# A transformer layer on one core: scans a block later, the second norm in steps, FFN's first blocks by halves

## The chip, the cores and the metric

The kernel runs on one core of one Trainium2 chip. The time is that of one execution on the device in microseconds (us). TensorE (PE) multiplies matrices, VectorE (DVE), ScalarE (ACT) and GpSimd (POOL) work element by element, and SyncE (SP) issues DMA transfers. Each has an in-order queue of its own, and a semaphore makes one wait for another.

## What is computed

One layer for 1024 latent tokens with a context of 256, width 1024, in fp32. The shift, scale and gate vectors come from a matrix `w_ada`.

```python
hc = modulate(rms_norm(ctx, norm1_gain), csh1, csc1)
feats_c, post_c = mixer_inputs(hc, w_in, mlstm_gate_bias, None)
ret_c, ml_c, st_f, st_b = bidirectional_scans(feats_c, log_gamma, zero, zero)
hx = modulate(rms_norm(x, norm1_gain), sh1, sc1)
feats_x, post_x = mixer_inputs(hx, w_in, mlstm_gate_bias, rope)
ret_x, ml_x, _, _ = bidirectional_scans(feats_x, log_gamma, st_f, st_b)
x = x + g1 * mixer_output(ret_x, ml_x, *post_x, w_ret_up, w_ml_up, w_out)
x = x + g2 * swiglu(modulate(rms_norm(x, norm2_gain), sh2, sc2), w_ffn_in, w_ffn_out)
return rms_norm(x, final_gain)
```

`bidirectional_scans` runs four retention heads and four mLSTM heads over chunks of 128 tokens, forwards and backwards. In the mLSTM scan, running sums and maxima of the gates i and log sigmoid(f) give three weights per token. `mixer_output` normalises each head's output, gates it, lifts both branches to the full width, merges them and applies `w_out`.

## The kernel before, in words

**Arithmetic.** Each fp32 operand is split into a high and a low part (ACT cast, L191; DVE subtraction, L192), and a product takes three matmuls. A PSUM bank holds 128x512. TensorE has two banks "ch", two "ts" for large products and four "sc" for small ones. Large products come in blocks of 256 weight columns by 1024 tokens. A Winograd scheme takes seven instead of eight quarter products (`winograd_block`, L276, seven steps); weight factors are made by POOL, DVE and ACT from `raw` tiles loaded by SP.

**Stages.** First the vectors from `w_ada` beside the first norm of the context (`scaled_tile`, L468) and the key and value products of the context (`ctx_tiles`, L442: four pairs of weight tiles, eight steps k each). `modulate_split` (L394) makes each tile of a norm twice: on ACT into the high part (L395), on POOL as the full value `tmp` (L396). DVE subtracts them into the low part (L397). Then 14 head blocks (u = 1 to 7 in two parts, u = 0 is plain) and 8 blocks of the merge gates (`wbg`) run in `run_blocks` (L320), which calls `tick` (L994) after each of a block's seven steps. `tick` moves generators on, registered with `beside(generator, rate)`; the rate is the number of yields a tick. They are `gates` (L691, the weights per token; it starts at u = 1), `scan(u)` (L805, one head; the first at u = 2, the last two in gate blocks 1 and 3), `ada2` (L972) and `load_y_ret` (L1059).

**A scan** is a list of slots. `load` fetches a chunk's keys and values (once per direction, 19 loads of 128 KB a scan), `decay` weights them on POOL (L838), `advance` (L852, L857) adds their product to the state, `stage_a`, `stage_b` and `stage_c` make the outputs of chunk j (L898 to L931) into tiles `o`. The squares of `o` are summed on ACT into a scratch tile `junk` (L933), `norm_y` (L941) normalises, `put_y` (L947) transposes and stores.

**After the scans.** Up products (L111 to L113), then the out product by halves of the tokens, `hf` 0 and 1, each followed by its second norm. Then the FFN: two plain blocks for group 0 (`w0` gate, `w1` up), with `right_factors` (L1161, L1166) on DVE for the Winograd blocks in between, then 20 Winograd blocks and the last product. POOL multiplies up by silu of gate into `hid` (L1158), and SP stores it (L1159) for the last product.

The program is written in this order, and the framework orders each engine's instructions from it.

## Time and profile before

| | |
|---|---|
| median of 3 runs | 1650.39 us (1649.82 to 1653.24) |
| profiled execution | 1655.51 us, span 1653.7 us |
| TensorE busy | 1578.3 us, 95% |
| DVE, ACT, POOL busy | 1003.5, 725.7, 460.2 us |
| mean granted clock of TensorE | 0.984 |

The span runs from the first instruction to the last; the execution's own time is 1.8 us longer. TensorE is busy in nearly all of it; from 740 to 900 us and from 1040 to 1500 us its matmuls follow one another without a gap.

### The profile page before, as it was taken

What the parts mean: (1) busy time and instruction counts of PE and PEld (TensorE: products, weight loads), DVE (VectorE), ACT (ScalarE), POOL (GpSimd) and SP (SyncE); (2) the same over time, 40 slices, a digit from 0 to 9 for tenths busy, and PEclk for the clock granted to TensorE, in tenths of its full rate; (3) what the DMA queues carried; (4) which work ended last, traced back from release to release, by engine and by line L of the source; (5) the groups of instructions that cost most, each with busy time, mean ns of one, the idle gap of its engine ahead of it and who ended that gap; (6) DMA issues with size and microseconds to landing.
All of it is one profiled execution on the core that took longest, in us unless ns stands there. A gap on an engine that the chain in (4) does not pass through costs nothing.

```text
span 1653.7 us, 22635 instructions
## 1 busy us (share of the span) xinstructions
PE 1578.3 (95%) x7478; PEld 1287.9 (78%) x7478; DVE 1003.5 (61%) x1841; ACT 725.7 (44%) x1404; POOL 460.2 (28%) x506
## 2 busy tenths in 40 slices
PE   7999978899999999999999999999999999999997
PEld 2677757787878788778888777888888888888886
DVE  4578786776767767765445677555555555536243
ACT  4655434544545566655223354434443334534230
POOL 0143216455344444410220226222222221001001
PEclk9999978999999999999999999999999999999998
DMA  8753537787767765546456312222232224835531
GB/s 293 255 159 104 167 105 234 252 258 240 248 210 218 228 202 180 187 141 215 154 162 202 122 56 96 81 92 84 85 96 87 77 90 155 271 96 179 171 96 52
DMA packets 188230, 264.55 MB, mean 160 GB/s; under 512 B 19232, under 2 KB 85920, under 8 KB 188112
## 3 DMA queue, kind: packets, MB, share of 16 engines
q1 hardware_dynamic: 186240, 260.99, 49.8%
q10 hardware_dynamic: 1872, 2.10, 0.4%
q8 instruction: 59, 0.97, 0.2%
q14 instruction: 59, 0.48, 0.1%
HBM read 206.64 MB, written 56.38 MB: 159 GB/s over the span
## 4 chain that ended last, share of the span: by engine, by line
PE 51%; POOL 2%; DVE 2%; DMA 1%; ACT 1%; issue 0%; DVEq 0%; SPq 0%; ACTq 0%
PE ch L258 15%; PE ts L258 12%; PE ch L1291 2%; PE ch L1292 2%; PE ch L1290 2%; PE ts L1290 2%; PE ts L1292 2%; PE ts L1291 2%; POOL hid L1158 1%; PE ts L113 1%; PE ch L113 1%; PE ts L112 1%; PE ts L111 1%; PE ch L111 1%; PE ch L112 1%; POOL xf L396 1%
## 5 line engine op out<-in xcount | busy, mean ns | idle before, releaser
L192 DVE TENSOR_TENSOR fw<-raw,fw 128x512 fp32r<-128x512 f32 x305 | 223.1, 737 | 156.6 <-ACT fw L191 156.1
L258 PE MATMUL ts<-A,fw 128*128 128x512 f32 x1200 | 300.7, 398 | 1.8 <-DVE A L397 0.9
L191 ACT CAST fw<-raw 128x512 fp32r<-128x512 f32 x305 | 188.0, 620 | 257.2 <-PE ch L1292 89.0
L258 PE MATMUL ch<-A,fw 128*128 128x512 f32 x1176 | 289.4, 394 | 0.0
L258 PEld LDWEIGHTS ts<-A,fw 128*128 128x128 f32 x1200 | 225.1, 191 | 50.9 <-DVE A L397 3.0
L258 PE MATMUL ch<-t,fw 128*128 128x512 f32 x1008 | 250.4, 396 | 5.5 <-ACT u L293 3.9
L258 PEld LDWEIGHTS ch<-A,fw 128*128 128x128 f32 x1176 | 219.5, 189 | 45.8 <-issue 1.0
L258 PEld LDWEIGHTS ch<-t,fw 128*128 128x128 f32 x1008 | 187.5, 189 | 44.7 <-ACT u L293 5.1
L1158 POOL TENSOR_TENSOR hid<-hid,sg 128x512 f32<-128x512 f32 x44 | 90.2, 2062 | 217.6 <-DVE hid L288 200.9
L258 PE MATMUL ts<-t,fw 128*128 128x512 f32 x504 | 129.6, 404 | 3.2 <-ACT fw L191 1.9
L293 ACT COPY u<-ch 128x512 f32<-128x512 f32 x104 | 60.9, 586 | 134.0 <-PE ch L258 133.7
L258 PEld LDWEIGHTS ts<-t,fw 128*128 128x128 f32 x504 | 95.6, 193 | 23.1 <-ACT fw L191 2.1
L192 DVE TENSOR_TENSOR fw<-stg,fw 128x512 fp32r<-128x512 f32 x126 | 94.5, 750 | 31.3 <-ACT fw L191 31.2
L230 POOL TENSOR_TENSOR stg<-raw,raw 128x512 f32<-128x512 f32 x42 | 63.5, 1513 | 156.2 <-DVE fw L192 100.4
L191 ACT CAST fw<-stg 128x512 fp32r<-128x512 f32 x126 | 78.6, 624 | 59.4 <-DVE stg L230 29.2
L838 POOL TENSOR_SCALAR vs<-kv,dcol 128x128 f32<-128x128 f32 x72 | 63.0, 882 | 63.1 <-DMA kv<-kv_d 33.0
L838 POOL TENSOR_SCALAR vs<-kv,colq 128x129 f32<-128x129 f32 x72 | 54.8, 762 | 78.5 <-PE sc L852 38.0
L1282 POOL TENSOR_SCALAR cp<-cp,cpack 128x256 f32<-128x256 f32 (+1 forms) x6 | 8.2, 1361 | 222.1 <-ACT stg L1336 222.1
L192 DVE TENSOR_TENSOR fw<-s,fw 128x512 fp32r<-128x512 f32 x42 | 33.4, 796 | 48.0 <-ACT fw L191 48.0
L983 DVE SCALAR_TENSOR_TENSOR acc<-stg,silu_c,acc 128x512 f32<-128x512 f32 x56 | 46.8, 836 | 18.2 <-DMA stg<-wada 18.1
L230 DVE TENSOR_TENSOR stg<-raw,raw 128x512 f32<-128x512 f32 x42 | 39.0, 930 | 27.1 <-DMA raw<-wffn 16.8
L396 POOL TENSOR_SCALAR t<-stg,a,sh 128x512 f32<-128x512 f32 (+1 forms) x24 | 27.3, 1144 | 95.8 <-issue 31.5
(362 smaller groups left out, 2973.3 us busy)
## 6 DMA issues: line engine op xcount, KB each, us to landing
raw<-wffn SPq DMA_DIRECT2D x88, 256.0 KB
raw<-wfo SPq DMA_DIRECT2D x88, 256.0 KB
kv<-kv_d SPq DMA_DIRECT2D x152, 128.0 KB
raw<-win SPq DMA_DIRECT2D x64, 256.0 KB
stg<-wada SPq DMA_DIRECT2D x64, 256.0 KB
hid_d<-hid SPq DMA_DIRECT2D x44, 256.0 KB
hraw<-hid_d SPq DMA_DIRECT2D x40, 256.0 KB
araw<-wada SPq DMA_DIRECT2D x32, 256.0 KB
```

What stands on the lines that cost most here:

```text
L191: nc.scalar.copy(hi, x)
L192: nc.vector.tensor_tensor(out=lo, in0=x, in1=hi.bitcast(F32), op=ALU.subtract)
L230: eng.tensor_tensor(out=o, in0=x, in1=y, op=op)
L258: nc.tensor.matmul(ps, lhsT=w[wp_][:, c], rhs=x[xp][k], start=start and k == i == 0, stop=cont or (stop and k == 3 and i == 2), skip_group ...
L293: nc.scalar.copy(o, chain)
L396: nc.gpsimd.tensor_scalar(out=tmp, in0=xn, scalar1=scale, scalar2=shift, op0=ALU.mult, op1=ALU.add)
L838: nc.gpsimd.tensor_scalar(out=vs, in0=kv[d, n][1], scalar1=col, scalar2=None, op0=ALU.mult)
L983: nc.vector.scalar_tensor_tensor(out=acc, in0=raw, scalar=s, in1=acc, op0=ALU.mult, op1=ALU.add)
L1158: nc.gpsimd.tensor_tensor(out=c, in0=c, in1=sgs[f, hf], op=ALU.mult)
L1290: nc.tensor.matmul(ps, lhsT=w[0][:, c], rhs=h[0][:, t], start=kt == 0, stop=False)
L1291: nc.tensor.matmul(ps, lhsT=w[0][:, c], rhs=h[1][:, t], start=False, stop=False)
L1292: nc.tensor.matmul(ps, lhsT=w[1][:, c], rhs=h[0][:, t], start=False, stop=kt == 2 * NG - 1)
```

## The change

The diff, cut to its core (`after` and `at` put a function at the end or the start of a scan's slot):

```diff
-    def modulate_split(xn, hi, lo, scale, shift, tmp):
+    def modulate_split(xn, hi, lo, scale, shift, tmp, beneath=False):
         nc.scalar.activation(hi, xn, AF.Identity, scale=scale, bias=shift)
-        nc.gpsimd.tensor_scalar(out=tmp, in0=xn, scalar1=scale, scalar2=shift, ...)
+        if beneath:
+            nc.scalar.activation(tmp, xn, AF.Identity, scale=scale, bias=shift)
+        else:
+            nc.gpsimd.tensor_scalar(out=tmp, in0=xn, scalar1=scale, scalar2=shift, ...)
...
-    ctx_order = [(p, k) for k in range(KT) for p in range(2)] + [(p, k) for p in (2, 3) for k in range(KT)]
+    ctx_order = ([(p, k) for k in range(6) for p in range(2)] + [(2, 0), (2, 1)] + [(p, k) for k in (6, 7) for p in range(2)]
+                 + [(2, k) for k in range(2, KT)] + [(3, k) for k in range(KT)])
...
-                    ctx_ps[pair, n] = mm_ps()
+                    ctx_ps[pair, n] = sc_ps() if pair == 2 else mm_ps()
...
+    for k_ in (0, 1):
+        ctx_tiles(2, (k_,))
+        ctx_load()
     for k_ in (6, 7):
         for pair in range(2):
             ctx_tiles(pair, (k_,))
...
-        nc.gpsimd.tensor_tensor(out=gi, in0=gi, in1=bb, op=ALU.subtract)
-        nc.gpsimd.tensor_tensor(out=bb, in0=bb, in1=m, op=ALU.subtract)
+        nc.vector.tensor_tensor(out=gi, in0=gi, in1=bb, op=ALU.subtract)
...
+        nc.vector.tensor_tensor(out=bb, in0=bb, in1=m, op=ALU.subtract)
...
+        for i, n in enumerate((0, 1, 9, 8, 7, 6, 5, 4, 3, 2)):
+            after(i // 2 if i < 9 else 6, load, n)
         for i, n in enumerate((1, 0, 9, 8, 7, 6, 5, 4, 3)):
-            after(i // 2, load, 1, n)
-            at(i // 2 + 2, decay, 1, n)
-            at(i // 2 + 3, advance, 1, n)
-        for n in range(NCH):
-            after(5 + n, load, 0, n)
-            if n < 9:
-                at(7 + n, decay, 0, n)
-                at(8 + n, advance, 0, n)
+            at(i // 2 + 3, decay, 1, n)
+            at(i // 2 + 4, advance, 1, n)
+        for n in range(9):
+            at(4 + n if n < 2 else 7 + n, decay, 0, n)
+            at(6 + n if n < 2 else 8 + n, advance, 0, n)
...
-            junk = bt([P, P], "junk", 1)
-            nc.scalar.activation(junk, raw, AF.Square, accum_out=ssq[:, j:j + 1])
+            nc.scalar.activation(po[:, 3 * P:], raw, AF.Square, accum_out=ssq[:, j:j + 1])
...
-            at(9 + j, stage_a, j)
-            at(10 + j, stage_b, j)
-            at(11 + j, stage_c, j)
-        at(20, norm_y)
-        at(23, put_y, 0)
-        at(24, put_y, 4)
+            at(10 + j, stage_a, j)
+            at(11 + j, stage_b, j)
+            at(12 + j, stage_c, j)
+        at(21, norm_y)
+        at(25, put_y, 0)
+        at(26, put_y, 4)
...
+    def norm_steps(hf, acc):
+        nc.vector.tensor_tensor(out=acc[0], in0=acc[0], in1=acc[1], op=ALU.add)
+        dg_ = rms_cols(acc[:1], 512)
+        yield
+        y = rms_bcast(dg_)
+        h2 = (slot_a(), slot_a())
+        hh.append(h2)
+        for kt in range(KT):
+            xr = xf[hf][:, kt, :]
+            nc.vector.tensor_tensor(out=xr, in0=y, in1=xr, op=ALU.mult)
+            modulate_split(xr, h2[0][:, kt, :], h2[1][:, kt, :], a2[:, kt:kt + 1], mod2[:, 8 + kt:9 + kt], xr)
+            if kt % 2:
+                yield
...
+                next(norm, None)
+        norm = norm_steps(hf, acc)
+    for _ in norm:
+        pass
...
+        if gidx == 0:
+            held_back.append((hid_d[f, hf], c))
+        else:
+            nc.sync.dma_start(hid_d[2 * gidx + f, hf], c)
...
+                while part == 1 and held_back:
+                    nc.sync.dma_start(*held_back.pop(0))
...
-    plain_block(w0, b_all, plain_copy("sg", lambda f, hf, c: gate_done(sgs, f, hf, c)))
+    plain_half(w0, b_all, 0, gate_copy)
+    plain_half(w1, b_all, 0, up_copy)
     for k in range(4):
         right_factors(k)
     seven_blocks = list(ffn_blocks())
+    plain_half(w0, b_all, 1, gate_copy)
     seven_blocks[0][0].load()
-    plain_block(w1, b_all, plain_copy("hid", lambda f, hf, c: up_done(0, sgs, f, hf, c)))
+    plain_half(w1, b_all, 1, up_copy)
```

Not in this cut: `gates` loads and biases the forget gates before the input gates and has some 23 yields instead of 18; the rates and starts (gates at u = 1, part 1, rate 1 for 0.85; scans from u = 3, rate 1.5 for 1.45, the last three in gate blocks 0, 2 and 4; `ada2` 0.68 for 0.95; `load_y_ret` at block 7, rate 1.6, for block 6, rate 1); a chunk is loaded once for both directions (10 loads a scan instead of 19) and the mask once in each mLSTM scan; tile "kv" has 9 buffers for 8, "sf" 4 for 3, "acc" 4 for 2; one more tile `wx` for the last weights of `w1`.

Three places show how it moves instructions. VectorE at the gates, before (L724 and L725 are the gates' scans; L582 and L579 belong to the rotation of keys and queries; fw, stg and s are weight parts):

```order
L582 SCALAR_TENSOR_TENSOR kt_1947<-wt_1953,kt_1947 128x512
L192 TENSOR_TENSOR fw_1980<-raw_1796,fw_1980 128x512
L192 TENSOR_TENSOR fw_2134<-raw_1983,fw_2134 128x512
L230 TENSOR_TENSOR stg_2137<-raw_1985,raw_1987 128x512
L230 TENSOR_TENSOR s_2142<-stg_2137,raw_1983 128x512
L192 TENSOR_TENSOR fw_2139<-stg_2137,fw_2139 128x512
L724 SCALAR_TENSOR_TENSOR g_1576<-g_1575,g_1574 4x1280
L725 SCALAR_TENSOR_TENSOR g_1573<-g_1574,g_1572 4x1280
L724 SCALAR_TENSOR_TENSOR g_1576<-g_1575,g_1574 4x256
L725 SCALAR_TENSOR_TENSOR g_1573<-g_1574,g_1572 4x256
L724 SCALAR_TENSOR_TENSOR g_1576<-g_1575,g_1574 4x1024
L725 SCALAR_TENSOR_TENSOR g_1573<-g_1574,g_1573,g_1572 4x1024
```

VectorE after the change at the same place, from the second half of the scans on (L755 and L757 are the scans, L764 and L768 POOL's two subtractions of before, L294, L593 and L594 a rotation):

```order
L597 SCALAR_TENSOR_TENSOR kt_1931<-wt_1937,kt_1931 128x512
L757 SCALAR_TENSOR_TENSOR g_1543<-g_1544,g_1543,g_1542 4x1024
L769 COPY gm_1549<-g_1543 4x9
L770 COPY gm_1549<-g_1543 4x1
L764 TENSOR_TENSOR g_1542<-g_1542,g_1546 36x1280
L771 COPY gm_1549<-g_1543 4x1
L772 COPY gm_1549<-g_1543 4x7
L768 TENSOR_TENSOR g_1546<-g_1546,g_1543 36x1280
L294 TENSOR_TENSOR kt_2027<-ts_2014,u_1916 128x512
L774 TENSOR_TENSOR g_1544<-g_1546,gm_1549 36x1280
L593 TENSOR_TENSOR kt_2027<-kt_2027,rp_2029 128x512
L294 TENSOR_TENSOR kt_2055<-ts_1978,wt_2053 128x512
```

The rotation sum L582 (now L597) and four of the instructions for weights that stood ahead of the first scan have gone behind it; between the scans and the sum kt_2055 stand the wide gate products.

TensorE at the first products of a scan's states, before (L852 the state product, L258 a step of a Winograd block):

```order
L258 MATMUL ch_2155<-t_1401,fw_2152 128x512
L258 MATMUL ch_2155<-t_1400,fw_2152 128x512
L258 MATMUL ch_2155<-t_1431,fw_2152 128x512
L258 MATMUL ch_2155<-t_1432,fw_2152 128x512
L852 MATMUL sc_2304<-vs_2257,kv_2220 128x128
L258 MATMUL ch_2155<-t_1431,fw_2152 128x512
L852 MATMUL sc_2307<-vs_2259,kv_2222 128x128
L564 MATMUL sc_2330<-cpack,kt_2204 128x128 x4
L852 MATMUL sc_2341<-vs_2310,kv_2246 128x128
L258 MATMUL ch_2155<-t_1478,fw_2152 128x512
L852 MATMUL sc_2344<-vs_2312,kv_2248 128x128
L258 MATMUL ch_2155<-t_1479,fw_2152 128x512
```

and after (L882 the state product, L265 the block):

```order
L265 MATMUL ts_2446<-t_1293,fw_2314 128x512
L265 MATMUL ts_2446<-t_1312,fw_2314 128x512
L265 MATMUL ts_2446<-t_1313,fw_2314 128x512
L265 MATMUL ts_2446<-t_1312,fw_2314 128x512
L882 MATMUL sc_2460<-vs_2422,kv_2365 128x128
L882 MATMUL sc_2463<-vs_2424,kv_2363 128x128
L882 MATMUL sc_2474<-vs_2466,kv_2395 128x128
L882 MATMUL sc_2477<-vs_2468,kv_2397 128x128
L265 MATMUL ch_2330<-t_1355,fw_2319 128x512
L265 MATMUL ch_2330<-t_1356,fw_2319 128x512
L265 MATMUL ch_2330<-t_1355,fw_2319 128x512
L265 MATMUL ch_2330<-t_1395,fw_2319 128x512
```

A state product stood by itself between two matmuls of a chain, and now several stand together between two chains.

SyncE's queue at the start of the FFN, before (raw are weight loads, hid_d the stores of hid, cp loads of x):

```order
L211 DMA raw_10352<-wffn 128x512
L1159 DMA hid_d<-hid_10197 128x512
L1325 DMA cp_13478<-x_d 128x512
L1325 DMA cp_13480<-x_d 128x512
L1325 DMA cp_13482<-x_d 128x512
L1325 DMA cp_13484<-x_d 128x512
L1159 DMA hid_d<-hid_10226 128x512
L211 DMA raw_10354<-wffn 128x512
L1159 DMA hid_d<-hid_10255 128x512
L211 DMA raw_10356<-wffn 128x512
```

and after:

```order
L211 DMA raw_10110<-wffn 128x512
L1236 DMA hid_d<-hid_9843 128x512
L1236 DMA hid_d<-hid_9871 128x512
L1378 DMA cp_13240<-x_d 128x512
L1378 DMA cp_13242<-x_d 128x512
L1378 DMA cp_13244<-x_d 128x512
L1378 DMA cp_13246<-x_d 128x512
L211 DMA raw_10112<-wffn 128x512
L1236 DMA hid_d<-hid_10015 128x512
L211 DMA raw_10114<-wffn 128x512
```

Two hid stores stand between the first and the second of these weight loads in both.

## Rows read from the trace of the kernel before

**Rows 1.** Windows: length, busy us (x) of PE, PEld, DVE, ACT, POOL, clock, DMA, GB/s.
```profile
216.00:231.50 15.50, 6.16 (x17) 4.50 (x15) 15.41 (x14) 3.58 (x5) 7.03 (x3) 0.67 0.02 3
238.00:245.00 7.00, 7.00 (x32) 5.72 (x32) 3.23 (x5) 4.15 (x15) 0.00 (x0) 0.51 0.47 128
261.00:266.00 5.00, 4.56 (x16) 3.70 (x17) 1.40 (x3) 0.17 (x1) 1.97 (x3) 0.66 1.05 381
272.00:279.00 7.00, 6.21 (x21) 5.45 (x22) 5.24 (x10) 1.93 (x4) 5.34 (x5) 0.51 0.82 262
```

**Rows 2.** Waits of PE, 40 to 120 us: for whom, us in total, times, longest.
```profile
PE ts L452 <- DVE fw L192: 1.9, 2, 1.2
PE ts L451 <- ACT t L395: 1.1, 1, 1.1
```

**Rows 3.** Groups of ScalarE by form: busy us, mean ns | idle before.
```profile
L395 ACT ACTIVATE A<-stg,sh,a 128x512 fp32r<-128x512 f32 x16 | 12.7, 814 | 7.9 <-DVE stg L473 7.8
```

**Rows 4.** Timeline of PE, 216 to 245 us: start, us, what, [idle before].
```profile
225.29 0.32 PE L768 MATMUL sc<-cpack,g 36*128 36x36 f32 x1 [8.91 <-POOL g L736]
...
236.43 0.89 PE L768 MATMUL sc<-cpack,g 36*128 36x36 f32 x11 [1.36 <-ACT g L751]
```

**Rows 5.** Timeline of VectorE, 200 to 240 us.
```profile
205.78 1.78 DVE L582 SCALAR_TENSOR_TENSOR kt<-wt,kt 128x512 f32<-128x512 f32 x1
...
211.05 2.81 DVE L724 TENSOR_TENSOR_SCAN g<-g,g 4x1280 f32<-4x1280 f32 x1 [0.23 <-DMA g<-ls_d]
...
219.96 2.31 DVE L725 TENSOR_TENSOR_SCAN g<-g,g,g 4x1024 f32<-4x1024 f32 x1
...
231.14 1.48 DVE L741 TENSOR_TENSOR g<-g,gm 36x1280 f32<-36x1280 f32 x1
```

**Rows 6.** Waits of PE, 255 to 320 us.
```profile
PE sc L947 <- DVE o L941: 3.5, 1, 3.5
PE sc L852 <- POOL vs L838: 2.2, 1, 2.2
PE ts L258 <- ACT fw L191: 1.9, 1, 1.9
PE sc L898 <- DMA qk<-qk_d: 1.5, 1, 1.5
```

**Rows 7.** Waits of PE, 320 to 722 us.
```profile
PE sc L947 <- DVE o L941: 5.9, 4, 1.8
PE sc L922 <- DVE sf L857: 4.7, 4, 2.6
PE sc L915 <- DVE sf L857: 3.6, 3, 1.4
```

**Rows 8.** Line 933 on ScalarE, the squares: ns min/median/max, and a releaser.
```profile
L933 ACT ACTIVATE junk<-o x64: 293/311/323, 279.0 to 714.4; 128x128 f32<-128x128 f32 x64
...
  POOL o L931: 17.3, 21
```

**Rows 9.** Line 931 on POOL, the gate product.
```profile
L931 POOL TENSOR_TENSOR o<-o,g x32: 454/460/892, 511.8 to 713.9; 128x128 f32<-128x128 f32 x32
```

**Rows 10.** Waits of PE, 900 to 1040 us.
```profile
PE ch L258 <- ACT u L293: 3.4, 1, 3.4
PE ts L113 <- DVE fw L192: 3.3, 1, 3.3
PE ts L258 <- DVE A L397: 0.9, 3, 0.3
PE ts L258 <- ACT A L395: 0.7, 1, 0.7
```

**Rows 11.** Chain that ended last, 905 to 1030 us: start, length, what.
```profile
992.18 21.54 POOL hid L1158 x3
...
1014.15 5.83 DMA raw<-wffn
```

**Rows 12.** Line 1158 on POOL: ns min/median/max, first and last start.
```profile
L1158 POOL TENSOR_TENSOR hid<-hid,sg x44: 1290/1696/18119, 992.2 to 1397.7; 128x512 f32<-128x512 f32 x44
```

More of the change, by code (lines that the diff above doesn't have):

```diff
@@ L212, in raw_quads, with plain_quads @@
         return r
-    def plain_quads(src):
+    def plain_quads(src, last=None):
         r = raw_quads(src)
-        return {k: parts_of(r[k]) for k in ("a11", "a21", "a12", "a22")}
+        w = {k: parts_of(r[k]) for k in ("a11", "a21", "a12")}
+        if last is None:
+            w["a22"] = parts_of(r["a22"])
+        else:
+            split(*last, r["a22"])
+            w["a22"] = last
+        return w
     class Factors:
@@ L708, in gates @@
         yield
-        log_sigmoid(pg, lso, lsx, [P, 80], "g")
-        nc.sync.dma_start(ls_d[1], lso)
-        for d in range(2):
-            nc.sync.dma_start(gf[32 * d:32 * d + H], rows[1][4 * d:4 * d + H])
+        biased(0, gi, gil)
         m, rm = gil, gfl
@@ L717, in gates @@
         nc.gpsimd.memset(rm[32:36, P - 1::P], 0.0)
+        yield
+        yield
+        yield
+        log_sigmoid(pg, lso, lsx, [P, 80], "g")
+        yield
+        nc.sync.dma_start(ls_d[1], lso)
+        for d in range(2):
+            nc.sync.dma_start(gf[32 * d:32 * d + H], rows[1][4 * d:4 * d + H])
+        yield
+        yield
         yield
@@ L783, in open_scans @@
         t = {}
-        t["mask"] = pb.tile([P, 2, P], F32, name="mask")
-        nc.sync.dma_start(t["mask"], a["mask"])
         t["g128"] = pb.tile([P, 2, H], F32, name="g128")
@@ L1022, in first @@
             def first():
-                if (u, part) == (1, 0):
-                    beside(gates(), 0.85)
-                if part == 0:
+                if part == 1:
                     return
-                if u == 2:
+                if u == 1:
+                    beside(gates())
+                if u == 3:
                     drain()
@@ L1030, in first @@
                     open_scans()
-                    beside(ada2(), 0.95)
-                if u >= 2:
-                    beside(scan(u - 2), 1.45)
+                    beside(ada2(), 0.68)
+                if u >= 3:
+                    beside(scan(u - 3), 1.5)
             return w, first, lambda: winograd_block(w, b_all, t_all, head_done(u, part), head_tile, snap_tile)
@@ L1112, in body @@
     hh = []
+    def norm_steps(hf, acc):
+        nc.vector.tensor_tensor(out=acc[0], in0=acc[0], in1=acc[1], op=ALU.add)
+        dg_ = rms_cols(acc[:1], 512)
+        yield
+        y = rms_bcast(dg_)
[6 more added lines that the diff above has]
+            if kt % 2:
+                yield
+    norm = iter(())
     out_w = ahead([a["wout"][i, kh] for _ in range(2) for i in range(4) for kh in range(2)])
     for hf in range(2):
-        acc = [px0.tile([P, 512], F32, tag="acc", bufs=2, name=nm("acc")) for _ in range(2)]
+        acc = [px0.tile([P, 512], F32, tag="acc", bufs=4, name=nm("acc")) for _ in range(2)]
         for i in range(4):
@@ L1200, in body @@
     w0 = plain_quads(a["wffn"][0, 0])
-    w1 = plain_quads(a["wffn"][0, 1])
+    wx = pe.tile([P, 2, 512], F32R, name="wx")
+    w1 = plain_quads(a["wffn"][0, 1], (wx[:, 0, :], wx[:, 1, :]))
     def plain_copy(tag, done):
```

113 lines of the change are left out of this document (57 added, 56 removed).

## The prediction

> **What bounds the kernel now.** TensorE is the bound, so the time changes only by what it loses to waits and to the lower clock. I read three views in this order. First the windows: they show stretches in which its busy time is short or the granted clock is near 0.5, the lower of the two levels (1.2 of 2.4 GHz), at which the same matmuls take twice as long [rows 1]. Half the time spent at that level is lost; the window at 261 us, for one, loses (1 - 0.66) x 5.0 = 1.7 us, and four more stretches of the same length, 3.4 us, begin at 64, 313, 931 and 1023 us. Then the waits of TensorE, by stage: who is late, how often, how long [rows 2, 4, 6, 7, 10]. Then the other engines' own rows at each place [rows 3, 5, 8, 9, 12] and the chain that ended last [rows 11]. A wait costs its own length plus half of the lower-clock stretch that follows it. Matmul work is the same before and after: no matmul is added or removed.
>
> All sums are made against the profiled execution, 1655.51 us. It stands 5.1 us above the median of the three runs (1650.39 us); a gain in the one is taken as the same gain in the other.
>
> **First norm and context products.** Before, TensorE waits 1.9 + 1.1 us for the first norm's tiles and the casts beside it [rows 2]. Behind the wait of 1.1 us lies the slow stretch at 64 us, 1.7 lost. The four context products (12 matmuls) moved ahead stand exactly behind that 1.1 us wait and cover it: 2.8 us back. Against that, ScalarE now makes the norm's tiles: 16 of 128x512 at 0.81 us [rows 3] (13 us) and 8 of 128x256, shorter than 0.81 each, in one queue with the weight casts for which TensorE already waited. POOL is relieved, but TensorE waited here for none of its products directly. I take 2 us of later casts. Bounds: nothing late (0) and half of the 13 us (6.5). **Net 1 us gained** (-4 to +3).
>
> **Gates.** In the window at 216 us TensorE works 6.2 of 15.5 us: 9.3 us idle, of which 8.9 are the wait for POOL's subtraction L736 [rows 1, 4]. The work after it, 225.3 to 231.2, is at half clock (3.0 us lost), then 1.4 us wait for an exponential of ScalarE [rows 4], then a second slow stretch, 7.0 us at 0.51 (3.4 us lost) [rows 1]. Sum 17.1 us. VectorE made the gates' six scans from 211.05 to 222.27 (219.96 + 2.31), 11.2 us without a gap [rows 5], and POOL's subtraction came after them. The change loads the forget gates first and takes both POOL subtractions to VectorE, where the nearest row with the same shape is 1.48 us [rows 5]. By the order, a rotation sum (L582, 1.78 us [rows 5]) and four instructions for weights (0.7 each, by the gap from it to the first scan) no longer stand ahead of the scans, so these begin 4.6 us earlier, near 206.5, if their loads have landed. But between the scans and the sum kt that the next transposes need, VectorE now has 11.2 + three wide products of 1.5 + four of 0.7 (rotation, kt itself among them) + 0.6 of small copies = 19 us: ready near 225.5, where TensorE arrives near 216.4 (225.29 - 8.91 [rows 4, 5]). So the wait changes its name rather than going: 8 to 9 us and one slow stretch of 3, against 17.1. **5 us gained.** Bounds: scans no earlier (211.05 + 19 = 230: 0 gained) and everything hidden but 3 us (14).
>
> **Onset of the scans.** Between 255 and 320 us the waits sum to 3.5 + 2.2 + 1.9 + 1.5 = 9.1 us [rows 6]; the slow stretches in the window at 261, in that at 272 (half of 6.2 busy us at 0.51) and at 313 lose 1.7 + 3.1 + 1.7 = 6.5 us [rows 1]. In total 15.6. After, scans begin one block later, key/value chunks are loaded once in the first slots, and a decay has three slots from the load instead of two; the small products come in groups of 3 or 4 between whole 12-chains instead of one between two matmuls. DMA has 80 loads of 128 KB instead of 152; their cost beside other work was nothing but the 1.5 us wait for a load [rows 6]. **14 us gained**, leaving 1.6 us. Bounds 8 and 15.6.
>
> **Scans, steady part.** From 320 to 722 us the three largest waits are for normalised outputs (5.9 us) and states (4.7 + 3.6 us), 14.2 together [rows 7]. Output waits had three slots between norm and transposes and get four, and the states have one slot and one buffer more. I count 9 of the 14.2 back. Against it stands the squares' new destination: the last quarter of the accumulator bank in place of a scratch tile. The bank now stays held for the square (0.3 us [rows 8]) and, in the four mLSTM scans, for POOL's gate product before it (0.46 us [rows 9]), for which ScalarE waited 0.8 us on average (17.3 us in 21 [rows 8]): 0.8 to 1.6 us longer for 32 mLSTM chunks, 0.3 us and a copy's wait for 32 retention chunks. Scans have four such banks, so most of it lies beside other products; I take 6 us, a fifth of 32 x 1. **Net 3 us gained.** Bounds +14 (no bank waited for) and -23 (each of 32 chunks waits 1 us, 9 back).
>
> By the Trainium skill (ScalarE: Activation LUTs, section "Step-by-step: what each stage is for"), PSUM is ScalarE's lower-latency destination, useful only if TensorE doesn't need most of PSUM. No row here shows the first half; the kernel gives TensorE two "ch", two "ts" and four "sc" banks, so its caveat speaks against this edit and for the third rival.
>
> **Between scans and second norm.** The retention outputs come back one block later at a higher rate; no wait stood there. **1 us lost** (0 to 3).
>
> **Second norm of half 0.** At 930 us a wait of 3.3 us [rows 10] and a slow stretch of 1.7: 5.0 us. Spread over the other half's eight steps, nothing waits for it until the FFN. The casts and multiplies go beside matmuls that last far longer. **5 us gained** (3 to 5).
>
> **FFN's first blocks by halves.** The second half's norm tiles have the first half's up product as cover, so the waits for A (0.9 + 0.7 us [rows 10]) go. The larger loss is later: POOL's first multiply of hid started at 992 and three of them took 21.5 us on the chain [rows 11], where the median of this line is 1.7 and the longest 18.1 [rows 12]; VectorE ran the right factors without a gap meanwhile. The hid stores stand on SP's queue ahead of a weight load (5.8 us), so TensorE waits 3.4 us [rows 10, 11] and loses 1.7 in the slow stretch behind it. The order of SP after the change still has two hid stores ahead of that load, and VectorE's run is the same, so the stall stays, and I allow 2 to 3 us of added wait because half 1's gate product now follows the norm as well. **Net 1 us lost.** Bounds: -3 and +7 (1.6 + 3.4 + 1.7 gone).
>
> The Trainium skill (SBUF — State Buffer, section "SBUF: two separate sides") says that VectorE with two SBUF inputs and GpSimd exclude each other for a whole instruction. The trace agrees where it shows it, 18.1 against 1.7 us for one instruction [rows 12]. If POOL came in between all the same, hid would be out in time and the 7 us would come.
>
> **Sum.** 1 + 5 + 14 + 3 - 1 + 5 - 1 = 26 us. The profiled execution would be 1655.5 - 26 = 1629.5 us; the median 1650.4 - 26 = **1624.4 us**.
>
> **Rivals.** (1) *The edits pay in full*: gates 14, scans 14, FFN 7, the rest as above: 1 + 14 + 14 + 14 - 1 + 5 + 7 = 54, less what no change can hide (two waits of 2 us and their clock, about 8): 46, or 1604 us. For it: every single wait named is one the change addresses. Against it: VectorE's queue at the gates and SP's order at the FFN. Chance 0.17. (2) *The waits are replaced*: casts late in the first norm (-4), gates 0, onset 8, steady part -8, FFN -3, norm 5, -1: 26 shrinks to about -3, and by parts between -3 and 10, or 1640 to 1653 us. For it: the same engines do the same work with more queued behind ScalarE and VectorE. Against it: the onset's single interleaved products clearly go. Chance 0.15. (3) *The held bank decides*: the squares in PSUM. If a chunk's chain to its square is longer than TensorE takes to come back to that bank, TensorE waits in each of the 32 mLSTM chunks. Without the 6 us counted for it the gain is 32, so 1.0 us each (32 x 1.0) uses it up. At 1.5 us each it is 48, and a slow stretch of 1.7 us after a fifth of them adds 11: 1650.4 - 32 + 59 = 1677 us. For it: the bank is held 0.8 to 1.6 us longer. Against it: four banks rotate. Chance 0.08. (4) *The held-back stores do not do what their name says*: this is in the forecast, since the order still has them ahead of the load; if they were behind it, 8 us more would come (7 in place of -1), or 1616; chance 0.05, within the forecast's 0.60.
>
> **How the numbers follow.** Chance of the forecast 0.60, its own range 1614 to 1636 (gates +-5, onset -5, steady part -6 to +5). The rivals 0.17, 0.15 and 0.08. The range 1600 to 1648 takes in most of the first two rivals and leaves out the third and the ends of these two, about 0.18. 0.2% is 3.3 us, about what a measurement of this kernel can tell from no change: faster by more than that 0.85 (forecast, rival 1 and half of rival 2), within it 0.05, slower 0.10 (rival 3 and the end of rival 2).
>
> **What would show it.** In the profile after: at 255 to 320 us no clock near 0.5 and waits under 3 us in sum (right), or waits for vs and o again (wrong). At the gates a wait of TensorE for kt of VectorE of 5 to 9 us in place of the 8.9 for POOL; if it is for POOL or gone, that step is wrong. In the scans no waits for o; a wait of the small products for the square, at more than 0.3 us a chunk, would be rival 3. At 930 clock 1.0 throughout. At the FFN the POOL multiply of hid again near 18 us and a wait for u of 3 to 6 us. In the first norm, waits for a cast. A time above 1648 would mean that waits have moved rather than gone; below 1600, that VectorE's queue at the gates was no limit.

## The result and the profile after

The changed kernel takes 1640.11 us (median of 4 runs, 1636.75 to 1641.78), the one before 1651.81 us on the same chip (median of 4, 1649.82 to 1653.24). The ratio is 0.9919, 95% interval 0.9903 to 0.9935: faster, by 11.7 us in the medians, where 26 were forecast. The forecast of 1624.4 us was too low by 15.7; the measured time lies in the stated range, 1600 to 1648. The profiled execution has a span of 1638.1 us against 1653.7 before, 15.6 us less. That is 4 us more than the medians give: the profiled execution of before, 1655.51 us, was 3.7 us slower than its median of four. The forecast had taken a gain in the one as the same gain in the other.

The stages of both, as windows (length, busy us (x count) of PE, PEld, DVE, ACT, POOL, clock, DMA share, GB/s). Before:

```profile
200.00:250.00 50.00, 39.31 (x170) 31.27 (x169) 40.91 (x49) 20.17 (x42) 11.88 (x8) 0.83 0.38 120
250.00:340.00 90.00, 79.43 (x412) 66.78 (x411) 63.76 (x122) 40.88 (x91) 52.70 (x54) 0.92 0.75 240
340.00:720.00 380.00, 360.92 (x2006) 306.50 (x2004) 270.93 (x651) 207.18 (x485) 167.50 (x285) 1.00 0.68 212
900.00:940.00 40.00, 36.62 (x155) 29.21 (x155) 28.09 (x52) 16.42 (x26) 9.25 (x8) 0.96 0.33 110
940.00:1060.00 120.00, 114.68 (x492) 91.89 (x491) 80.91 (x128) 51.94 (x88) 44.20 (x20) 0.99 0.28 89
```

After:

```profile
200.00:250.00 50.00, 40.36 (x195) 32.68 (x194) 43.04 (x53) 23.30 (x46) 12.46 (x9) 0.90 0.52 155
250.00:340.00 90.00, 78.50 (x399) 65.01 (x398) 62.09 (x117) 41.49 (x90) 46.25 (x48) 0.96 0.70 216
340.00:720.00 380.00, 367.41 (x2042) 312.03 (x2041) 268.32 (x640) 209.31 (x488) 162.49 (x251) 1.00 0.64 194
900.00:940.00 40.00, 40.00 (x181) 32.85 (x179) 29.04 (x55) 18.17 (x29) 8.58 (x8) 1.00 0.43 132
940.00:1060.00 120.00, 114.32 (x488) 92.81 (x487) 83.01 (x129) 53.65 (x92) 51.20 (x21) 0.97 0.25 77
```

What TensorE loses in a window is its idle time (length less busy) and what the clock takes, (1 - clock) x length; the clock has two digits, so the second is good to some tenths of a microsecond in the short windows and not at all in the one of 380 us, which has no slow stretch to speak of in either.

| us lost | before | after | gained | forecast |
|---|---|---|---|---|
| gates, 200 to 250 | 10.7 + 8.5 | 9.6 + 5.0 | 4.6 | 5 |
| onset, 250 to 340 | 10.6 + 7.2 | 11.5 + 3.6 | 2.7 | 14 |
| scans, 340 to 720 | 19.1 | 12.6 | 6.5 | 3 |
| second norm, 900 to 940 | 3.4 + 1.6 | 0 | 5.0 | 5 |
| FFN's start, 940 to 1060 | 5.3 + 1.2 | 5.7 + 3.6 | -2.8 | -1 |

The forecast's window for the onset ended at 320; it is 340 here, because the scans now begin a block later and what follows their start reaches to 335. In the first 120 us the loss falls by 1 to 2 us (11.8 + 1.2 to 11.5), where 1 was forecast. All terms but one came out within a few us. The onset gave 3 us in place of 14. In a second profile of the changed kernel (the first run below) the onset loses 13.5 us and the scans 15.3, so these two gains are 2.7 to 4.3 and 3.8 to 6.5 us. Where the border lies matters: by the forecast's own windows, 255 to 320 and 320 to 722 us, about 8 us are gained in the first and 1 in the second, because a wait of 4 us at 329 us then counts with the scans. Together it is 8 to 9 us either way, where 17 were forecast.

TensorE's waits after, in three stretches, set beside those of [rows 4], [rows 6] and [rows 7]. Between 200 and 250 us:

```profile
PE ch L265 <- ACT wt L299: 9.6, 1, 9.6
```

Between 250 and 340 us:

```profile
PE sc L882 <- DVE wt L979: 4.1, 1, 4.1
PE sc L946 <- DVE W L930: 2.8, 2, 2.6
PE sc L882 <- POOL vs L868: 2.1, 2, 1.7
PE sc L579 <- DVE kt L294: 1.3, 1, 1.3
```

Between 340 and 720 us:

```profile
PE sc L882 <- DVE sf L887: 3.8, 3, 1.7
PE sc L952 <- DVE W L932: 2.4, 4, 0.7
...
PE sc L944 <- DVE sf L887: 1.1, 1, 1.1
...
PE sc L975 <- DVE o L969: 0.2, 1, 0.2
```

Of the waits of the onset before [rows 6], those for the load of queries, for o and for weight casts have gone. In their place TensorE waits 4.1 us for VectorE's product in a store of outputs (L979) and 2.8 for a weighted product W (L930); the wait for vs is still there, 2.1 us in two where it was 2.2 in one. Along the scans, in the forecast's window, the waits for o have fallen from 5.9 to 0.2 us and those for states from 8.3 to 4.9 (L882 and L944). That is the 9 us for which the extra slot and buffer were counted; no run takes these two away by themselves.

### The profile page after: what moved, and what is told of

Read it like the earlier page. It is cut to its first block, busy times and chain, and to the rows that moved or that the text cites. A ratio compares the mean times of both kernels' runs of the same rounds, so it can differ in the third digit from the quotient of the medians.

```text
span 1638.1 us, 22335 instructions
## 1 busy us (share of the span) xinstructions
PE 1571.9 (96%) x7478; PEld 1282.6 (78%) x7478; DVE 999.9 (61%) x1843; ACT 740.6 (45%) x1430; POOL 427.2 (26%) x444
## 4 chain that ended last, share of the span: by engine, by line
PE 63%; DVE 8%; DMA 6%; issue 4%; ACT 3%; POOL 3%; SPq 0%; DVEq 0%; POOLq 0%; ACTq 0%
PE ch L265 20%; PE ts L265 15%; PE ch L1345 2%; PE ch L1344 2%; PE ch L1343 2%; PE ts L1343 2%; PE ts L1345 2%; PE ts L1344 2%; DMA stg<-wada 2%; PE ch L113 1%; PE ts L113 1%; PE ch L111 1%; PE ts L112 1%; PE ch L112 1%; PE ts L111 1%
## 5 line engine op out<-in xcount | busy, mean ns | idle before, releaser
L192 DVE TENSOR_TENSOR fw<-raw,fw 128x512 fp32r<-128x512 f32 x304 | 225.0, 745 | 145.9 <-ACT fw L191 145.1
L265 PE MATMUL ts<-A,fw 128*128 128x512 f32 x1200 | 295.3, 394 | 0.6 <-DVE kt L294 0.6
L265 PE MATMUL ch<-A,fw 128*128 128x512 f32 x1152 | 282.1, 393 | 9.6 <-ACT wt L299 9.6
L265 PE MATMUL ch<-t,fw 128*128 128x512 f32 x1008 | 254.2, 400 | 7.1 <-ACT u L299 5.5
L265 PEld LDWEIGHTS ts<-A,fw 128*128 128x128 f32 x1200 | 222.4, 188 | 46.4 <-DVE kt L294 1.6
L265 PEld LDWEIGHTS ch<-A,fw 128*128 128x128 f32 x1152 | 214.9, 188 | 55.2 <-ACT wt L299 10.2
L265 PEld LDWEIGHTS ch<-t,fw 128*128 128x128 f32 x1008 | 189.9, 191 | 47.4 <-ACT u L299 6.8
L1201 POOL TENSOR_TENSOR hid<-hid,sg 128x512 f32<-128x512 f32 x44 | 95.5, 2182 | 214.9 <-DVE hid L294 202.4
L299 ACT COPY u<-ch 128x512 f32<-128x512 f32 x104 | 60.8, 585 | 147.9 <-PE ch L265 147.8
L265 PE MATMUL ts<-t,fw 128*128 128x512 f32 x504 | 126.8, 399 | 0.0
L192 DVE TENSOR_TENSOR fw<-stg,fw 128x512 fp32r<-128x512 f32 x126 | 95.2, 755 | 40.2 <-ACT fw L191 39.9
L265 PEld LDWEIGHTS ts<-t,fw 128*128 128x128 f32 x504 | 95.4, 192 | 19.3
L868 POOL TENSOR_SCALAR vs<-kv,dcol 128x128 f32<-128x128 f32 x72 | 54.7, 770 | 54.6 <-PE sc L882 37.6
L591 POOL TENSOR_TENSOR wt<-wt,rp 128x512 f32<-128x512 f32 x16 | 28.8, 1800 | 152.4 <-ACT wt L590 140.4
L192 DVE TENSOR_TENSOR fw<-s,fw 128x512 fp32r<-128x512 f32 x42 | 30.6, 728 | 53.6 <-ACT fw L191 53.6
L1011 DVE SCALAR_TENSOR_TENSOR acc<-stg,silu_c,acc 128x512 f32<-128x512 f32 x56 | 47.7, 852 | 21.0 <-DMA stg<-wada 20.9
L882 PE MATMUL sc<-vs,kv 128*128 128x128 f32 (+1 forms) x288 | 47.5, 281 | 11.8 <-DVE wt L979 4.9
```

The costliest lines, as they stand in the source:

```text
L192: nc.vector.tensor_tensor(out=lo, in0=x, in1=hi.bitcast(F32), op=ALU.subtract)
L265: nc.tensor.matmul(ps, lhsT=w[wp_][:, c], rhs=x[xp][k], start=start and k == i == 0, stop=cont or (stop and k == 3 and i == 2), skip_group ...
L299: nc.scalar.copy(o, chain)
L868: nc.gpsimd.tensor_scalar(out=vs, in0=kv[n][1], scalar1=col, scalar2=None, op0=ALU.mult)
L882: nc.tensor.matmul(ps, lhsT=kv[n][0], rhs=vsd.pop((d, n)), start=True, stop=True)
L1011: nc.vector.scalar_tensor_tensor(out=acc, in0=raw, scalar=s, in1=acc, op0=ALU.mult, op1=ALU.add)
```

## Where the onset's time goes

The two long waits of the onset lie behind VectorE's queue. The wait for W, on the timeline of VectorE and POOL (start us, us, line, out<-in, [idle before]):

```profile
288.47 1.71 POOL L591 TENSOR_TENSOR wt<-wt,rp 128x512 f32<-128x512 f32 x1
288.98 1.75 DVE L593 TENSOR_TENSOR kt<-kt,rp 128x512 f32<-128x512 f32 x1
290.65 0.28 DVE L930 TENSOR_TENSOR W<-sc,dt 128x128 f32<-128x128 f32 x1
```

W itself (L930) takes 0.28 us. It stands behind a rotation product of the keys, L593, that took 1.75 us beside POOL's L591, where the median of L593 is 0.7. TensorE had ended the product that W needs by 284.6 us, so L593 is only the last of what lay ahead of W: between the two VectorE also worked off two weight parts, a sum of the second norm's vectors and two smaller steps. TensorE stood 2.6 us. The wait for wt, 39 us later, with TensorE's side of it:

```profile
323.92 1.04 PE L975 MATMUL sc<-cpack,o 128*128 128x128 f32 x8
329.73 0.76 PE L882 MATMUL sc<-vs,kv 128*128 128x128 f32 x4 [4.09 <-DVE wt L979]
```

```profile
321.91 1.23 DVE L1011 SCALAR_TENSOR_TENSOR acc<-stg,silu_c,acc 128x512 f32<-128x512 f32 x1
322.55 1.75 POOL L591 TENSOR_TENSOR wt<-wt,rp 128x512 f32<-128x512 f32 x1
323.06 1.78 DVE L596 SCALAR_TENSOR_TENSOR kt<-kt,rp 128x512 f32<-128x512 f32 x1
324.77 0.74 DVE L1011 SCALAR_TENSOR_TENSOR acc<-stg,silu_c,acc 128x512 f32<-128x512 f32 x1
325.43 0.68 DVE L597 SCALAR_TENSOR_TENSOR kt<-wt,kt 128x512 f32<-128x512 f32 x1
325.58 1.65 POOL L237 TENSOR_TENSOR stg<-raw,raw 128x512 f32<-128x512 f32 x1 [1.29 <-DVE acc L1011]
326.03 1.75 DVE L1011 SCALAR_TENSOR_TENSOR acc<-stg,silu_c,acc 128x512 f32<-128x512 f32 x1
...
329.00 1.27 DVE L979 TENSOR_TENSOR wt<-sc,g 128x512 f32<-128x512 f32 x2
```

The two products L979 empty the PSUM banks of the scan's transposed outputs, which the next scan's first state products need. TensorE had transposed them by 325.0. VectorE came to them at 329.0, behind two halves of a rotation (L596, L597), three sums for the second norm's vectors (L1011) and two weight parts. Again two of the instructions beside POOL take 1.75 and 1.78 us rather than 0.7. In the kernel before the two stores' transposes came 4 us apart, at 312.02 and 316.26, with four of the next scan's state products and six matmuls of the block between them; now all eight stand together and the next scan's products right behind them.

From this come two theories. **V**: the waits are due to VectorE's queue at the first scans, which holds the rotation, the second norm's sums and weight parts, and the later start only moves them. **S**, the third rival of the forecast: the squares' hold on the PSUM bank takes the gain.

## Experiments

All edits are made to the changed kernel. The expectations count a loss from the distances of matmul starts and name 15 to 18 us for the onset of the changed kernel; by idle time and clock, as in the table and in all that follows, it is 13.5 to 15.1. The two profiles of the changed kernel differ by 1.6 us in the onset and by 2.7 along the scans, so up to 3 us in one stretch of one profile are no finding by themselves. Every run is a ratio to the kernel before, timed on the same chip, and is held against the changed kernel's two, 0.9919 and 0.9930; where a difference is given as a span of us, it is against these two.

**The changed kernel again.** No edit.

> The changed kernel itself, for comparison on the same chip. It should repeat 0.992 of the kernel before. In its profile, what TensorE loses between 255 and 340 us (waits and the lower clock) should again be 15 to 18 us, in waits for VectorE (a product W, a store's product wt) and POOL; if those waits come and go between executions, they are chance and no cause.

Measured 1641.86 us, ratio 0.9930 [0.9914, 0.9947]. These waits repeat in place and length: wt 3.5 us, vs 2.8, W 2.5, and 9.6 at the gates; the one of 1.3 for kt does not. The window 250 to 340 loses 9.9 + 3.6 us. The long waits are no chance.

**The squares in SBUF.**

```diff
-            nc.scalar.activation(po[:, 3 * P:], raw, AF.Square, accum_out=ssq[:, j:j + 1])
+            junk = bt([P, P], "junk", 1, mybir.dt.bfloat16)
+            nc.scalar.activation(junk, raw, AF.Square, accum_out=ssq[:, j:j + 1])
```

> The changed kernel with the squares written to an SBUF scratch tile again (16-bit, for space) instead of the outputs' own PSUM bank. Theory S (the squares' hold on the bank takes the gain): 4 to 10 us shorter than the changed kernel. Theory V (VectorE's and POOL's queues at the first scans take it): within 3 us, and between 250 and 340 us again 14 to 18 us lost.

An fp32 scratch tile, as the kernel before has it, finds no room in the changed kernel: the scans' pool would need 37.5 KB of each partition, and 37.3 are left. Measured 1639.21 us, ratio 0.9928 [0.9913, 0.9944], like the changed kernel. The same waits for wt (3.1), W (2.6) and vs (1.5) stand in the onset, and one for kt (2.5). Theory S falls: the bank's hold costs nothing that the time can show. In the changed kernel TensorE's waits behind a square are these, from the view of its line on ScalarE (ns min/median/max of one; who waited, us in all, times):

```profile
L961 ACT ACTIVATE sc<-o x64: 262/281/283, 289.3 to 723.5; 128x128 f32<-128x128 f32 x64
...
  PE sc L927: 0.4, 1
  PE sc L951: 0.2, 1
```

Its matmuls waited 0.6 us in all, where 6 were counted.

**Fewer sums on VectorE.**

```diff
                 if kt == 0:
                     nc.vector.tensor_scalar(out=acc, in0=raw, scalar1=s, scalar2=None, op0=ALU.mult)
-                else:
-                    nc.vector.scalar_tensor_tensor(out=acc, in0=raw, scalar=s, in1=acc, ...)
```

> The changed kernel without seven of eight accumulations of the second norm's vectors on VectorE (56 instructions of 0.84 us); their loads stay, the vectors are wrong by what is left out. Theory V (the scans' waits moved to VectorE's queue, which is full while the first scans run): the 15 to 18 us lost between 255 and 340 us fall below 8, and the time is 8 to 14 us shorter than the changed kernel's. Theory S (the squares' hold on PSUM banks takes the gain): the loss stays, time within 3 us.

Measured 1631.46 us, ratio 0.9865 [0.9851, 0.9880], 10.4 us less than the changed kernel in the same set. The time is as theory V had it, the place is not: the onset still loses 8.1 + 3.6 us, with a wait of 2.4 us for wt and now one of 3.9 for kt. That is 2 to 3 us less than the changed kernel's, and along the scans 1.5 to 4 are gained. VectorE's load matters, but thinning it by these sums does not free the onset, and where all of the 10 us lie its one profile does not show.

**Scans one head earlier.**

```diff
-                if u == 3:
+                if u == 2:
                     drain()
...
-                if u >= 3:
-                    beside(scan(u - 3), 1.5)
+                if u >= 2:
+                    beside(scan(u - 2), 1.5)
...
-                if blk in (0, 2, 4):
-                    beside(scan(2 * H - 3 + blk // 2), 1.5)
+                if blk in (0, 2):
+                    beside(scan(2 * H - 2 + blk // 2), 1.5)
```

> The changed kernel with the scans starting one head earlier again (u = 2, the last two in gate blocks 0 and 2), all else kept, loads of a chunk once among it. If the later start is what gave the onset its gain: 5 to 8 us longer than the changed kernel, with waits between 240 and 300 us. If the gain came from the loads and slots: within 2 us.

Measured 1644.40 us, ratio 0.9941 [0.9921, 0.9960], against 0.9930 [0.9914, 0.9947]: the intervals overlap, and the time is 2 to 4 us longer. In its profile the three windows from 200 to 720 us lose 10.9 + 5.0, 7.6 + 1.8 and 16.3 us, 41.6 in all; the changed kernel loses 42.3 and, run again, 43.4. The later start by itself is worth nothing that shows. Against before (19.2 + 17.8 + 19.1 = 56.1) the other scan and gate edits are left to have made the difference. The run is not quite clean: its start lies two blocks ahead of the changed kernel's, one ahead of the start before, and what is left of the gates is then written out in one go.

**Outputs copied by ScalarE.**

```diff
+                nc.scalar.copy(sy, py)
-                nc.vector.tensor_tensor(out=sy, in0=py, in1=g, op=ALU.mult)
+                nc.vector.tensor_tensor(out=sy, in0=sy, in1=g, op=ALU.mult)
```

> The changed kernel with the retention scans' transposed outputs copied out of PSUM by ScalarE first, and multiplied by the gate on VectorE afterwards (8 more ScalarE copies of 0.6 us). Theory V: the wait of 3.5 to 4.1 us near 329 us and the one of 0.8 us later go, with their slow stretch of 1.7: 4 to 7 us shorter. If only the whole load of VectorE counts and not where an instruction stands in its queue: no shorter than 2 us.

Measured 1634.90 us, ratio 0.9906 [0.9889, 0.9922], 2 to 4 us less, which is not clear of the noise. The wait for wt is gone from the onset, but the one for vs is 4.5 us instead of 2.1 and the one for sf 1.7 instead of 0.6; the window loses 8.4 + 3.6 us. So the place in VectorE's queue is what made this wait, and 3.5 of its 4.1 us come back as others.

**Weightings on ScalarE.**

```diff
-            nc.gpsimd.tensor_scalar(out=vs, in0=kv[n][1], scalar1=col, scalar2=None, op0=ALU.mult)
+            nc.scalar.activation(vs, kv[n][1], AF.Copy, scale=col)
```

> The changed kernel with the 144 weightings of a scan's values on ScalarE in place of POOL. If POOL's lateness and its exclusion of VectorE make the onset's waits: the waits for vs (2.1 to 2.8 us) go and those for W and wt shrink, 250 to 340 us lose 5 to 9 us less, the time falls by 4 to 9 us. If ScalarE's queue is the next bound (its copies of chain results stand behind the weightings): as much is lost in waits for ScalarE, time within 3 us or longer.

Measured 1638.41 us, ratio 0.9917 [0.9897, 0.9937]. The waits for vs and W go; the one for wt stays (3.1), the one for sf grows from 0.6 to 2.5, 1.9 us are idle ahead of state products for no cause that the profile shows, and the window loses 8.6 + 3.6. POOL is not the cause of most of it: its busy time in this window fell from 46 to 24 us and the time by no more than the uncertainty.

**Without the last head's rotation.**

```diff
-                    later(1, rotate, c, hf, QSCALE if part else None)
+                    if u != 3:
+                        later(1, rotate, c, hf, QSCALE if part else None)
```

> The changed kernel without the rotation of head u = 3's keys and queries (four tiles: 8 VectorE, 4 POOL and 8 ScalarE instructions and 8 loads less), the last head that is rotated, beside which the first scan now runs; that part of the result is left out. If the onset's loss comes from the rotation standing in the queues between the scan's instructions: 250 to 340 us lose 8 us or less instead of 16 to 18, the time is 7 to 11 us shorter. If the scan's own chain (product, VectorE, product) makes the waits: 13 us or more remain, within 4 us.

Measured 1627.63 us, ratio 0.9852 [0.9836, 0.9869], 11 to 13 us less than the changed kernel. The onset:

```profile
250.00:340.00 90.00, 84.73 (x453) 71.04 (x451) 62.58 (x121) 40.64 (x90) 42.80 (x49) 1.00 0.67 210
```

TensorE loses 5.3 us with no slow stretch. VectorE is busy as long as in the changed kernel (62.6 us here, 62.1 there): other work has moved into the place of the eight instructions, so its busy time does not tell why TensorE waits less. The waits for W (0.5 in two) and wt are gone. Only the waits for vs (2.5 us in two) and one for a weight load (1.3) are longer than 0.5. The two halves of the rotation alone:

```diff
+        if how == 1:
+            sw = sn
+        else:
             nc.scalar.copy(sw[0:64], c[64:P])
             nc.scalar.copy(sw[64:P], c[0:64])
             nc.gpsimd.tensor_tensor(out=sw, in0=sw, in1=sn, op=ALU.mult)
+        if how == 2:
+            return
```

with `how` 1 for u = 3 in the one and 2 in the other.

> The changed kernel with the rotation of head u = 3 cut to its eight VectorE instructions and its loads; the ScalarE copies and POOL products are left out. If VectorE's queue holds the scan: 250 to 340 us lose 13 us or more, time as the changed kernel's (1636 to 1642). If ScalarE and POOL do: 8 to 10 us, as without the rotation, 1626 to 1630.

> The changed kernel with the rotation of head u = 3 cut to its ScalarE copies, POOL products and loads; the eight VectorE instructions are left out. If VectorE's queue holds the scan: 8 to 10 us lost between 250 and 340 us, 1626 to 1631. If ScalarE and POOL do: 13 us or more, 1636 to 1642.

Measured 1631.04 us, ratio 0.9869 [0.9842, 0.9896], and 1630.93 us, 0.9874 [0.9846, 0.9902]. The same window, first with VectorE's part alone, then without it:

```profile
250.00:340.00 90.00, 83.73 (x438) 69.91 (x437) 64.03 (x126) 38.84 (x87) 42.37 (x47) 0.98 0.74 231
```

```profile
250.00:340.00 90.00, 83.98 (x446) 70.23 (x445) 62.49 (x117) 44.82 (x96) 47.79 (x50) 1.00 0.75 234
```

They lose 8.1 and 6.0 us, and the times are 8 to 10 and 7 to 9 us less than the changed kernel's. Neither half makes the 13.5 to 15.1 us, and neither theory of one engine holds: with the whole rotation of this head the stretch loses 13.5 to 15.1, with either half alone 6 to 8, without it 5. The wait for W is 0.2 us in both. The one for wt differs, first with VectorE's part alone, then without it:

```profile
PE sc L887 <- DVE wt L984: 1.3, 1, 1.3
```

```profile
PE sc L887 <- DVE wt L984: 3.3, 1, 3.3
```

In the second, VectorE has nothing of this rotation left to do and is late all the same, behind sums and weight parts, two of which took 1.75 and 1.78 us beside POOL. So the wait for W needs both halves, and the one for wt hangs more on the half of ScalarE and POOL, as far as one profile of each can tell.

How the halves act together is read from rows, not shown. The rotation goes from ScalarE's copies over POOL's product to VectorE's sum, and VectorE, which takes its instructions in order, can stand before that sum with the scan's products behind it. For this head it does so three times in the changed kernel's onset:

```profile
277.58 0.69 DVE L594 TENSOR_TENSOR kt<-kt,wt 128x512 f32<-128x512 f32 x1 [2.34 <-POOL wt L591]
310.21 0.69 DVE L596 SCALAR_TENSOR_TENSOR kt<-kt,rp 128x512 f32<-128x512 f32 x1 [0.69 <-ACT wt L590]
312.08 0.69 DVE L597 SCALAR_TENSOR_TENSOR kt<-wt,kt 128x512 f32<-128x512 f32 x1 [1.18 <-POOL wt L591]
```

Behind the first of them TensorE waited 1.3 us for kt, in one of the two profiles. But these 4.2 us do not lie right ahead of the two long waits: there VectorE went from one instruction to the next, but for 0.36 us for a load, and what the rotation added was its own instructions, L593 of 1.75 us, L596 of 1.78 and L597 of 0.68. That leaving out the rotation takes 8 to 10 us of loss from the onset is shown; how much of it is VectorE's standing, how much the length of its queue and how much the stretched products was not taken apart.

**Gates spread.**

```diff
                 nc.vector.tensor_tensor_scan(out=v(bb), ...)
                 yield
+                yield
+                yield
                 nc.vector.tensor_tensor_scan(out=v(m), ...)
                 if not (d and i == 0):
                     yield
+                    yield
+                    yield
```

> The changed kernel with two more yields after each of the gates' scans, so that VectorE's sum kt stands two instructions (one wide product of 1.5 us, small copies) further on, behind one wide product instead of two. If VectorE's queue at the gates makes the wait of 9.6 us that TensorE has behind a ScalarE copy: the wait is 7 to 8.5 us, 1 to 3 us shorter in all. If the exponential on ScalarE makes it: unchanged at 9.6.

Measured 1636.14 us, ratio 0.9902 [0.9887, 0.9917], 3 to 5 us less, at the edge of the noise. The wait behind the ScalarE copy fell to 8.2 us, where it is 9.6 in both profiles of the changed kernel, and 0.7 came for kt. It follows VectorE's queue and not the exponential: in both kernels ScalarE had ended the exponential and stood idle for kt, 2.96 us in the changed kernel and 0.94 here.

**First norm's tiles on POOL again.**

```diff
-        modulate_split(xn, hi, lo, a1[:, kt, w:w + 1], sh1[:, kt, w:w + 1], xr[kt], True)
+        modulate_split(xn, hi, lo, a1[:, kt, w:w + 1], sh1[:, kt, w:w + 1], xr[kt])
```

> The changed kernel with the first norm's tiles made by POOL again. By the forecast the 24 ScalarE instructions cost 2 us in late casts and the moved context products gain 2.8: without them 0 to 120 us should lose some 9 to 10 us instead of 12, with waits for ScalarE casts gone. If ScalarE is not late: within 1 us, or longer by waits for POOL.

Measured 1637.49 us, ratio 0.9911 [0.9897, 0.9926]. TensorE is busy 108.7 of the first 120 us against 108.5. Its waits for ScalarE's casts (2.0 us in the changed kernel) go, and those for VectorE's weight parts (L192) grow from 0.8 to 2.4. The 24 instructions change the name of the wait and not its length.

**The hid stores on POOL's queue.**

```diff
-            held_back.append((hid_d[f, hf], c))
+            nc.gpsimd.dma_start(hid_d[f, hf], c)
```

> The changed kernel with the four hid stores of group 0 issued by POOL behind its own multiplies, so that SyncE's queue no longer has them ahead of weight loads. If the stores on that queue are what keeps the FFN's stall: the wait of 3.4 us for u near 1006 us and its slow stretch (1.7) go, 4 to 6 us shorter. If the weight products on VectorE are late in any case: the wait of 1.8 us near 996 us grows instead, within 2 us.

Measured 1631.75 us, ratio 0.9881 [0.9865, 0.9897], 6 to 8 us less than the changed kernel. The second of its two waits for u, 3.4 us, is gone. The POOL multiply in the changed kernel, the timeline of POOL:

```profile
971.69 26.78 POOL L1201 TENSOR_TENSOR hid<-hid,sg 128x512 f32<-128x512 f32 x3 [5.98 <-ACT hid L1255]
```

and here, where the instructions stand apart:

```profile
969.54 23.39 POOL L1201 TENSOR_TENSOR hid<-hid,sg 128x512 f32<-128x512 f32 x1 [4.94 <-ACT hid L1255]
993.23 0.58 POOL L1203 DMA_DIRECT2D hid_d<-hid  x1 [0.31 <-POOL hid L1201]
```

One multiply, 1.3 us by itself, took 23.4 us beside VectorE's run of right factors. It ended at 992.9, right after the first idle stretch of VectorE that the view lists since 964 us:

```profile
992.48 0.99 DVE L192 TENSOR_TENSOR fw<-stg,fw 128x512 fp32r<-128x512 f32 x1 [0.69 <-ACT fw L191]
```

The kernel before (18.1 us, to 1010.3, VectorE idle to 1009.8) and the changed one (23.4 us, VectorE idle to 994.6) show the same. The multiply is as late as ever, but nothing on SyncE's queue stands behind it any more. By idle time and clock 940 to 1060 us loses 2.0 + 1.2 us instead of 5.7 + 3.6.

**Combined.** The diffs of three runs above: hid stores on POOL's queue, outputs copied by ScalarE, gates spread.

> The changed kernel with three edits together: hid stores of group 0 on POOL's own queue, retention outputs copied out by ScalarE, gates spread. If the gains add: 8.5 + 4 + 2, some 12 to 15 us shorter than the changed kernel, 0.984 to 0.986 of the kernel before. If they share the same waits, 8 to 10.

Measured 1627.19 us, ratio 0.9849 [0.9834, 0.9863]: it beats both kernels, the changed one by 12 to 13 us. The onset still loses 8.5 + 5.4 us; the gains are in the FFN and along the scans.

With the diffs of two more, weightings on ScalarE and first norm's tiles on POOL:

> The three edits of the combined kernel, and with them the weightings on ScalarE and the first norm's tiles on POOL again. By single runs these two gave 3 and 1 to 3 us: if they add, 1622 to 1625 us, with 250 to 340 us losing 12 to 14 us. If the rotation's instructions hold the same stretch in any case: 1626 to 1629, no better than the combined kernel.

Measured 1631.89 us, ratio 0.9860 [0.9826, 0.9893], no better than the combined kernel that its wide interval could show.

## Why the prediction was right or wrong

The bound was read rightly: the matmuls are the same 7478, and the time fell by what TensorE lost less.

- **First norm and context products** (1 us): about 1 us was gained. The 2 us charged for late ScalarE casts are there, as waits of 2.0 us, but tiles on POOL again bring as much for VectorE, so ScalarE is not what sets them.
- **Gates** (5 us): 4.6. The wait did change its name, and VectorE's queue was the reason: its scans began at 204.62 (near 206.5 forecast) and the sum that the rotation needs was ready at 222.0 (225.5 forecast), behind two wide products. But TensorE waited at another place than I said, for ScalarE's copy of a chain, which stood behind rotation copies that waited for VectorE:

```profile
204.62 2.80 DVE L755 TENSOR_TENSOR_SCAN g<-g,g 4x1280 f32<-4x1280 f32 x1
...
219.89 1.48 DVE L768 TENSOR_TENSOR g<-g,g 36x1280 f32<-36x1280 f32 x1
221.30 0.68 DVE L294 TENSOR_TENSOR kt<-ts,u 128x512 f32<-128x512 f32 x1
```

```profile
217.78 1.27 ACT L763 ACTIVATE g<-g 36x1280 f32<-36x1280 f32 x1 [8.77 <-DVE g L757]
222.01 0.62 ACT L589 COPY wt<-kt 64x512 f32<-64x512 f32 x1 [2.96 <-DVE kt L294]
...
223.28 0.58 ACT L299 COPY wt<-ch 128x512 f32<-128x512 f32 x1
```

The forecast named kt at the transposes (L579); the copy (L299) is the same chain one engine further.
- **Onset** (14 us): this is the step that failed. It measured 2.7 and 4.3 us; 1.6 us were to be left, and 13.5 to 15.1 are. By the forecast's own window, to 320, it measured 8, its lower bound, and the wait at 329 spoils the next term. Its own sign of being wrong came in part: the waits from 255 to 320 sum to 6.8 us instead of under 3, those for vs among them, but none is for o. The step took every wait by the name it had in the trace of before, and counted it as gone when loads came earlier and the small products stood in groups. The waits for loads and for weight casts did go. The others were waits for VectorE and POOL, whose work in that stretch the change leaves nearly as it is (VectorE busy 63.8 us before and 62.1 after, POOL 52.7 and 46.3), and they came back under other names, with one of them in slots that the change itself put together (the two stores of a scan before the next one's first products). The lower bound of 8 had no row behind it: the trace gave no reason that the same work on VectorE in the same order of rotation, sums and scans would be on time a block later. Leaving out the rotation of the last head gives 8 to 10 us there; the later start gives none in the sum from 200 to 720 us.
- **Steady part** (3 us): 6.5 in one profile, 3.8 in the other (15.3 us idle). The waits for o and the states went by 9 us as counted, in the forecast's window; the 6 us charged for the squares' bank are 0.6. These two together would be some 8 us, so that the term came out near 3 is luck: other losses, the wait of 4 us at 329 among them in the forecast's window, took the rest.
- **Between scans and second norm** (-1): nothing shows. **Second norm** (5): 5.0, clock 1.00 and no wait at 930.
- **FFN by halves** (-1): about -3. The stall stayed for the reason given, POOL's multiply beside VectorE's run and the stores ahead of a weight load, and the added wait is 1.8 us (5.2 us in two waits for u, 3.4 before). The waits for A went, as forecast. The fourth rival's condition, stores off that queue, was made in a run and gave 6 to 8 us where 8 were priced.

Of the rivals the second (waits replaced) came nearest in mechanism, but for one stage only. The 15.7 us that the forecast was too low are these: 10.4 by which the profiles' gain falls short of 26, the onset above all; 3.9 by which that gain overstates the medians', since the profiled execution of before was a long one; and 1.4 because the median of before is 1651.81 and not 1650.39. The measured time lies outside the forecast's own range, 1614 to 1636, and at the edge of the second rival's, 1640 to 1653; the range of 1600 to 1648 holds it because it was drawn to take in most of that rival.

By the Trainium skill (SBUF — State Buffer, section "SBUF: two separate sides") a VectorE instruction with two SBUF inputs and a GpSimd instruction that reads SBUF shut each other out for a whole instruction. The multiply of 23.4 us beside VectorE's run agrees, and so do the VectorE products of 1.75 us beside POOL, though none of these runs shows by which port.

## What to carry to other kernels

Here a wait on a busy engine's in-order queue was not removed by moving the waiting stage. Ask what stands on that queue ahead of the instruction, and whether the change takes that away. Price such a stage by what the other engines still have to do in it, not by the names of its waits. A store that waits for a slow engine should not stand on the queue that brings the next weights: taking it off gave 6 to 8 us.
